# Whole-block transposes of the attention weights inside a matmul half, in a fused attention and recurrent block

## The chip, the cores and the metric

The kernel runs on one core of a Trainium2 chip. The metric is the device time of one execution in microseconds. The core has a matrix engine (TensorE: PE for its matmuls, PEld for its weight loads), three engines for elementwise work (VectorE: DVE, ScalarE: ACT, GpSimd: POOL), a queue engine (SP) that mainly issues DMAs, an on-chip memory (SBUF) of 128 partitions, and an accumulation memory (PSUM) of eight banks. TensorE writes to PSUM alone; DVE and ACT read it.

## The reference

The input is a residual stream of 2048 positions by 1024 channels, all in float32. One projection of 1024 to 9216 columns gives queries, keys and values of 24 heads, gates, and the input of a recurrence. Branch A is causal attention in three groups of eight heads: each query sees the keys of its own block of 128 and of the block before, with the positions regrouped by residue for dilations 1, 4 and 16.

```python
s = jnp.einsum('brnqhd,brnkhd->brnhqk', qb, kw) * (Dh ** -0.5)
s = jnp.where(valid[None, None, :, None], s, NEG_INF)
m = jnp.max(s, axis=-1, keepdims=True)
p = jnp.exp(s - m)
l = jnp.sum(p, axis=-1, keepdims=True)
o = jnp.einsum('brnhqk,brnkhd->brnqhd', p, vw)
...
wts = jax.nn.softmax(jnp.stack(lses, axis=0), axis=0)
attn = jnp.sum(wts[..., None] * jnp.stack(outs, axis=0), axis=0)
...
y_a = attn @ w_attn_proj[l]
...
y_b = (h * jax.nn.silu(g_lru)) @ w_lru_proj[l]
merged = gates[:, :, 0] * y_a + gates[:, :, 1] * y_b
out = merged @ w_out[l] + b_out[l]
x = layer_norm(DEEPNORM_ALPHA * x + out, ln_gain[l], ln_bias[l])
```

Branch B is a convolution, a gated linear recurrence over the positions, and a projection, y_b.

## The kernel before, in words

The kernel has three stages: the input projection with everything that is elementwise behind it; a loop of 49 steps ("groups") with the attention, into which the y_b projection is woven; and the rest of y_b, y_a, the output projection and the normalisation. The change lies in the middle loop alone.

The attention has 12 units (a pair of heads of one dilation), each with 16 query blocks. A block m has, for each of its two heads, a score tile of 128 queries by 256 keys; where a block has no block before it only 128 keys are used. All blocks but the first of dilation 1, and all but the first four of dilation 4, have 256; those of dilation 16 have 128. The prediction calls a group whose blocks have 256 a full group and one with 128 a half group. A group G takes four blocks, 4G to 4G+3, as two pairs, j = 2G and 2G+1. Its steps:

- `scores(j)` (matmul at L975): queries times keys for two blocks and both heads. The two heads lie on the lower and upper 64 partitions, so each matmul has 64 rows. The result goes to two banks of PSUM, tags s0 and s1, two buffers of each.
- `weigh(m)`: for each head a DVE instruction (L987) adds the mask, negates, and takes the extreme, and an ACT instruction (L989) makes the exponential and its sum. The weights p lie in an SBUF tile with eight places.
- `turn_p(j)` (L1003): TensorE transposes p, since the sums need the keys on the partitions. Each 128x128 block is turned in two halves of 64 queries; the halves go to two banks of PSUM, tags t0 and t1, one buffer of each. `copy_p(j, e)` takes a bank to SBUF: t0 on ACT (L1016), t1 on DVE (L1018), or on ACT in groups with spreads for the second pair.
- `values(js)` (L1035): the sums of p times v for two pairs, with 64 columns of the array for each head, into one bank (tag o, one buffer); DVE copies it to the unit's output (L1051).
- `yb_part(n, hf, i)` (L1205): three of the 12 matmuls, 128 by 128 by 512, of one half of the y_b projection's tile n; from group 4 on there is a half in each group but two (the groups after tiles 7 and 15).
- `spread(hp, c, g, tag)` (L1129): a matmul that spreads the shares of the three dilations over the partitions, whose result DVE multiplies into the outputs (o<-o,w). There are 36 in the loop, up to two in a group, in the banks t1 and t0.
- `turn_ml(u)` (L1056): in every fourth group, a transpose of a unit's extremes and sums (128 by 128, bank o), copied by ACT.

Each engine runs its instructions in the order in which the program issues them; semaphores hold an instruction until its inputs are there and its output's buffer has been read. So the order of the calls in the loop is the order on every engine. In a group of before it is: turn of pair 2G-2 (weighed in the group before), scores of 2G, two weighings, scores of 2G+1, turn of 2G-1, two weighings, the sums of pairs 2G-3 and 2G-2, then the y_b half with the spreads inside it.

The transposes of v in the first stage (L366) are whole 128x128 blocks, four to a bank, between the 128x512 matmuls of the projection (L633).

Of the kernel before, what the change touches and what calls it, by code (L numbers as in the profile page):

```python
# [8 lines left out]
F32 = mybir.dt.float32  # L9
F32R = mybir.dt.float32r  # L10
AF = mybir.ActivationFunctionType
# [4 lines left out]
P = 128  # L16
# [15 lines left out]
def hybrid_block_kernel(ctx: ExitStack, tc: tile.TileContext, a: dict, out: bass.AP):  # L32
# [27 lines left out]
    ident = cst.tile([P, P], F32, name="ident")  # L60
# [39 lines left out]
    cur = {}  # L100
# [14 lines left out]
    def run(queue):  # L115
        due = [x for x in queue if x[0] <= now["n"]]
        queue[:] = [x for x in queue if x[0] > now["n"]]
        for _, fn in due:
            fn()
# [806 lines left out]
    def gt(name):  # L926
        return rc_p.tile([P, CH], F32, tag="gt", name=name, bufs=3)
# [50 lines left out]
    def weigh(m):  # L978
        u, n = divmod(m, 16)
        bank, lo = st.pop(("s", m))  # L980
        if n == 0:
            ML[u] = at_p.tile([P, P], F32, tag="ml", name=f"ml{u}", bufs=2)
            pool.memset(ML[u][:, 64:P], 0.0)
        p = PT[:, m % 8]
        for h in range(2):
            mm, ll = (ML[u][:, 32 * k + 16 * h + n:32 * k + 16 * h + n + 1] for k in range(2))
            dve.tensor_tensor_reduce(out=p[:, h, lo:256], in0=bank[h][:, m % 2, lo:256], in1=mask[:, lo:256],  # L987
                                     scale=1.0, scalar=3e38, op0=ALU.add, op1=ALU.min, accum_out=mm)
            act.activation(p[:, h, lo:256], p[:, h, lo:256], AF.Exp, scale=-1.0, bias=mm, accum_out=ll)  # L989
        st["p", m] = (p, lo)  # L990

    def turn_p(j, tag="t"):

        pt = [aps.tile([P, 2, 4, 64], F32, tag=f"{tag}{e}", name=f"pt{e}{j}", bufs=1 if tag == "t" else 2) for e in range(2)]
        ptb = at_p.tile([P, 2, 4, P], F32, tag="pt", name=f"ptb{j}", bufs=3)
        los = []
        for b in range(2):
            p, lo = st.pop(("p", 2 * j + b))
            los.append(lo)
            for h in range(2):  # L1000
                for x in range(lo // P, 2):
                    for e, hs in enumerate((lo_, up_)):
                        pe.transpose(pt[e][:, b, 2 * h + x, :], p[hs, h, x * P:(x + 1) * P], ident[hs, hs])  # L1003
        st["t", j] = (ptb, pt, los)

    def copy_p(j, e):
        ptb, pt, los = st["t", j]
        on_act = e == 0 or (j % 2 and (j + 1) // 2 in spreads)
        whole = los[0] == los[1]
        for b in (slice(0, 2),) if whole else (slice(0, 1), slice(1, 2)):  # L1010
            lo = los[b.start]
            dst, src = ptb[:, b, :, 64 * e:64 * e + 64], pt[e][:, b]
            if lo:
                dst, src = (t.rearrange("p b (h x) f -> p b h x f", x=2)[:, :, :, 1, :] for t in (dst, src))
            if on_act:
                act.activation(dst, src, AF.Copy)  # L1016
            else:
                dve.tensor_copy(dst, src)  # L1018

    def values(js, tag="o"):  # L1020
        o = aps.tile([P, 4, P], F32, tag=tag, name=f"o{js[0]}", bufs=2 if tag == "s0" else 1)
        out = []
        for i, j in enumerate(js):
            u, n0 = divmod(2 * j, 16)
            g, _ = unit(u)
            V = AT_X["v"][:, u % 2]
            ptb, _, los = st.pop(("t", j))
            for b in range(2):
                n = n0 + b
                pv = prev(g, n)  # L1030
                lo = los[b]
                for x in range(lo // P, 2):
                    kb = n if x else pv
                    for h, hs in enumerate((lo_, up_)):
                        pe.matmul(o[hs, 2 * i + b, :], V[:, kb, 64 * h:64 * h + 64], ptb[:, b, 2 * h + x, :],  # L1035
                                  start=(x == lo // P), stop=(x == 1))
            if out and out[-1][0] == u and g != 1:
                out[-1][3] += 2
            else:
                out.append([u, n0, 2 * i, 2])  # L1040
        for u, n0, i, m in out:
            g, _ = unit(u)
            dst = o_tile(u)
            if g == 0:
                dst = dst.rearrange("p (n j) -> p n j", j=P)[:, n0:n0 + m]
            elif g == 1:
                c, r = divmod(n0, 4)
                dst = dst[:, c * CH:(c + 1) * CH].rearrange("p (j r) -> p r j", r=4)[:, r:r + m]
            else:
                dst = dst.rearrange("p (j r) -> p r j", r=16)[:, n0:n0 + m]  # L1050
            dve.tensor_copy(dst, o[:, i:i + m])  # L1051
# [72 lines left out]
    def spread(hp, c, g, tag):  # L1124

        cs = slice(c * CH, (c + 1) * CH)
        os = [o_tile(3 * hp + UG[x])[:, cs] for x in range(3)]
        w = cur["ps"].tile([P, CH], F32, tag=tag, name=f"w{hp}{c}{g}", bufs=cur["wb"])
        pe.matmul(w, sel[:, c // 2, g], WH[c % 2], start=True, stop=True)  # L1129
        tt(dve, os[g], os[g], w, ALU.mult)  # L1130
        if g == 0:
            st["ga", hp, c] = rc(f"ga{hp}{c}")
            sp.dma_start(st["ga", hp, c], ga_scr[hp * P:(hp + 1) * P, cs])
            return

        def join():
            tt(pool, os[0], os[0], os[g], ALU.add)
            if g == 1:
                tt(pool, os[0], os[0], st.pop(("ga", hp, c)), ALU.mult)
                if hp == 3 and c == CO[0]:  # L1140
                    later(1, lambda: split(AT[c][:, 3, 0], AT[c][:, 3, 1], os[0]))
                else:
                    pool.dma_start(at_scr[hp * P:(hp + 1) * P, cs], os[0])

        later(1, join)
# [47 lines left out]
    def yb_part(n, hf, i):  # L1193
        c, f = divmod(n, 8)
        if hf == 0 and i == 0:
            YB["t"] = cur["ps"].tile([P, CH], F32, tag="y", name=f"yb{c}{f}", bufs=cur["yb"])
        w = WL[:, n % 2]
        ks = range(4 * hf, 4 * hf + 4)
        if f == 0 or hf:
            order = [(k, a, b) for k in ks for a, b in ((0, 0), (0, 1), (1, 0))]  # L1200
        else:
            order = [(k, 0, b) for k in ks for b in range(2)] + [(k, 1, 0) for k in ks]
        for m in range(3 * i, 3 * i + 3):
            k, a, b = order[m]
            pe.matmul(YB["t"], w[:, a, k], hx(8 * c + k)[:, b], start=(hf == 0 and m == 0), stop=(hf == 1 and m == 11))  # L1205
# [38 lines left out]
            sp.dma_start(ME[c][:, f], yb_scr[f * P:(f + 1) * P, cs])  # L1244
        YG[i] = ga

    cur.update(wb=1, yb=1, ga=lambda i: gt(f"gA{i}"))
    GY = 4
    halves = list(range(64))
    NG = 48  # L1250
# [56 lines left out]
            spreads.setdefault(e + 7 + (i + (hp < 2)) // 2, []).append((hp, c, g))  # L1307

    rests = set()
    for G in range(NG + 1):  # L1310
        run(late)
        if G < NG:
            if G:
                turn_p(2 * G - 2)
                copy_p(2 * G - 2, 0)
                copy_p(2 * G - 2, 1)
            scores(2 * G)
            weigh(4 * G)
            weigh(4 * G + 1)
            scores(2 * G + 1)  # L1320
            if G:
                turn_p(2 * G - 1)
                copy_p(2 * G - 1, 0)
                copy_p(2 * G - 1, 1)
            weigh(4 * G + 2)
            weigh(4 * G + 3)
            if G:
                values([j for j in (2 * G - 3, 2 * G - 2) if j >= 0])
        else:
            turn_p(2 * G - 2)  # L1330
            copy_p(2 * G - 2, 0)
            copy_p(2 * G - 2, 1)
            turn_p(2 * G - 1, "s")
            copy_p(2 * G - 1, 0)
            copy_p(2 * G - 1, 1)
            values([2 * G - 3, 2 * G - 2])
            values([2 * G - 1], "s0")
        for fn in todo.pop(G, ()):
            fn()
        y = G >= GY and G not in rests and (G < NG or len(halves) % 2)  # L1340
        if y:
            n, hf = divmod(halves[0], 2)
            yb_part(n, hf, 0)
            yb_part(n, hf, 1)
        two = spreads.pop(G, [])
        if len(two) == 2:
            spread(*two[0], "t1")
        if y:
            yb_part(n, hf, 2)
        if two:  # L1350
            spread(*two[-1], "t0")
        if y:
            yb_part(n, hf, 3)
            if hf:
                yb_done(n)
        if G % 4 == 0 and G:
            turn_ml(G // 4 - 1)
        if y:
            yb_care(halves.pop(0))
            if hf and n in (7, 15):  # L1360
                rests.add(G + 1)
        now["n"] += 1
    assert not todo and not spreads, (todo, spreads)
    now["n"] += 1
    run(late)
# [269 lines left out]
```

## Time and profile before

| | |
|---|---|
| median of 3 runs | 2123.78 us (2121.55 to 2124.33) |
| the profiled execution's own time | 2123.79 us |
| its span | 2122.0 us |
| TensorE matmul rows busy | 2099.0 us, 11637 instructions |
| DVE, ACT, POOL busy | 1660.3, 1216.8 and 764.2 us |
| the loop: first scores to the last ml transpose | 1452.6 to 1785.2 us |
| transposes of p in the loop | 1200 rows |

All rows come from one profiled execution. In the lists by line, a row names line, engine, operation, tiles (out<-in), the array rows by columns and the moving operand, and then the count, busy time, mean length of one and the idle time before it. In the order of time a row is start, length, engine, line and so on, with instructions of one kind that follow each other put together. A matmul's length is its latency; several are in flight at a time, so what matmuls cost is read from the starts. A scores or sums matmul has two rows in the trace, a transpose one.

### The profile page before, as it was taken

What the parts mean: (1) busy time and instruction counts of PE and PEld (TensorE: products, weight loads), DVE (VectorE), ACT (ScalarE), POOL (GpSimd) and SP (SyncE); (2) the same over time, 40 slices, a digit from 0 to 9 for tenths busy, and PEclk for the clock granted to TensorE, in tenths of its full rate; (3) what the DMA queues carried; (4) which work ended last, traced back from release to release, by engine and by line L of the source; (5) the groups of instructions that cost most, each with busy time, mean ns of one, the idle gap of its engine ahead of it and who ended that gap; (6) DMA issues with size and microseconds to landing.
All of it is one profiled execution on the core that took longest, in us unless ns stands there. A gap on an engine that the chain in (4) does not pass through costs nothing. (4 is left out here: it accounts for less than half of the span.)

```text
span 2122.0 us, 34703 instructions
## 1 busy us (share of the span) xinstructions
PE 2099.0 (99%) x11637; PEld 1721.6 (81%) x11637; DVE 1660.3 (78%) x2938; ACT 1216.8 (57%) x2502; POOL 764.2 (36%) x692
## 2 busy tenths in 40 slices
PE   9999999999999999999999999999999999999998
PEld 7888888888888888888888888887878788788886
DVE  8787987988989767787677878775777777787667
ACT  6456456467457556677677777676666675321100
POOL 1554654654744301120110111113557678522120
PEclk9999999999999999999999999999999999999999
DMA  7876976976876966676666676769889886774431
GB/s 228 256 222 187 272 225 206 265 224 210 264 230 216 301 189 182 190 206 179 194 199 183 189 229 184 214 194 273 204 214 237 226 229 187 236 240 153 155 99 70
DMA packets 277505, 443.49 MB, mean 209 GB/s; under 512 B 64352, under 2 KB 116608, under 8 KB 274256
## 3 DMA queue, kind: packets, MB, share of 16 engines
q1 hardware_dynamic: 260688, 408.84, 62.8%
q0 software_dynamic: 11744, 23.54, 6.1%
q10 hardware_dynamic: 4896, 8.92, 1.1%
q8 instruction: 92, 1.51, 0.3%
q14 instruction: 85, 0.70, 0.1%
HBM read 290.00 MB, written 151.19 MB: 208 GB/s over the span
## 5 line engine op out<-in xcount | busy, mean ns | idle before, releaser
L633 PE MATMUL q<-xT,hS 128*128 128x512 f32 x1632 | 504.7, 390 | 0.0
L633 PE MATMUL q<-xT,l 128*128 128x512 f32 x1088 | 423.5, 389 | 0.0
L633 PE MATMUL q<-xB,hA 128*128 128x512 f32 x1344 | 417.2, 392 | 0.0
L633 PE MATMUL q<-xB,l 128*128 128x512 f32 x944 | 367.7, 389 | 0.0
L633 PEld LDWEIGHTS q<-xT,hS 128*128 128x128 f32 x1632 | 304.8, 188 | 64.4 <-issue 1.8
L633 PEld LDWEIGHTS q<-xB,hA 128*128 128x128 f32 x1344 | 250.3, 188 | 56.5 <-issue 5.5
L633 PEld LDWEIGHTS q<-xT,l 128*128 128x128 f32 x1088 | 204.3, 188 | 42.5
L236 POOL TENSOR_TENSOR sw<-sw,sin 128x512 f32<-128x512 f32 x96 | 156.1, 1632 | 167.7 <-ACT sw L325 74.0
L633 PEld LDWEIGHTS q<-xB,l 128*128 128x128 f32 x944 | 177.2, 188 | 37.0
L989 ACT ACTIVATE pt<-pt,ml 128x256 f32<-128x256 f32 (+1 forms) x384 | 172.2, 452 | 25.4 <-DVE ml L987 25.4
L236 POOL TENSOR_TENSOR y<-y,h 128x512 f32<-128x512 f32 x28 | 39.1, 1398 | 384.0 <-DVE h L535 368.0
L633 PE MATMUL q<-xB,hS 128*128 128x512 f32 x544 | 168.7, 391 | 1.1 <-DVE v L236 1.1
L633 PE MATMUL q<-xT,hA 128*128 128x512 f32 x544 | 167.9, 390 | 0.0
L280 ACT ACTIVATE hA<-wA 128x512 fp32r<-128x512 f32 x220 | 138.6, 635 | 29.2 <-DVE l L236 11.6
L1205 PE MATMUL yb<-hx,wl 128*128 128x512 f32 x576 | 149.5, 400 | 1.0 <-POOL hx L1181 0.8
L280 ACT ACTIVATE hS<-S 128x512 fp32r<-128x512 f32 x170 | 108.4, 638 | 66.0 <-DVE S L236 47.0
L236 POOL TENSOR_TENSOR l<-wA,hA 128x512 fp32r<-128x512 f32 x68 | 110.1, 1618 | 86.4 <-ACT hA L280 52.5
L1205 PEld LDWEIGHTS yb<-hx,wl 128*128 128x128 f32 x576 | 104.5, 188 | 29.9 <-issue 5.8
L987 DVE CUSTOM_DVE_ANT_0 pt<-s,mask 128x256 f32<-128x256 f32 (+1 forms) x384 | 115.6, 361 | 5.1 <-PE s L975 2.9
L633 PEld LDWEIGHTS q<-xT,hA 128*128 128x128 f32 x544 | 101.8, 188 | 21.7 <-issue 0.4
L633 PEld LDWEIGHTS q<-xB,hS 128*128 128x128 f32 x544 | 101.2, 188 | 22.4 <-issue 1.9
L324 ACT ACTIVATE sw<-y 64x512 f32<-64x512 f32 x96 | 60.6, 631 | 80.6 <-DVE y L577 78.7
(209 smaller groups left out, 4332.1 us busy)
## 6 DMA issues: line engine op xcount, KB each, us to landing
wA<-in_w_in_dram SPq DMA_DIRECT2D x220, 256.0 KB
wl_scr<-l SPq DMA_DIRECT2D x102, 512.0 KB
l<-wl_scr SPq DMA_DIRECT2D x102, 512.0 KB
wS<-in_w_in_dram SPq DMA_DIRECT2D x102, 256.0 KB
wS<-in_w_in_dram POOLq DMA_DIRECT2D x68, 256.0 KB, 6.8
wlr<-in_w_f_dram SPq DMA_DIRECT2D x64, 256.0 KB
mg_scr<-y SPq DMA_DIRECT2D x59, 256.0 KB
v_scr<-vs SPq DMA_DIRECT2D x48, 260.0 KB
```

The lines of the kernel that those rows point to most:

```text
L236: eng.tensor_tensor(out=out, in0=in0, in1=in1, op=op)
L280: act.activation(heads(h), heads(r, False), AF.Copy)
L324: act.activation(flat(sw)[lo_], flat(rw)[up_], AF.Copy, scale=scale)
L633: pe.matmul(bank, w[:, ks], x[:, kk, xx], start=(first and i == 0), stop=(last and i == 11))
L987: dve.tensor_tensor_reduce(out=p[:, h, lo:256], in0=bank[h][:, m % 2, lo:256], in1=mask[:, lo:256], scale=1.0, scalar=3e38, op0=ALU.add, o ...
L989: act.activation(p[:, h, lo:256], p[:, h, lo:256], AF.Exp, scale=-1.0, bias=mm, accum_out=ll)
L1205: pe.matmul(YB["t"], w[:, a, k], hx(8 * c + k)[:, b], start=(hf == 0 and m == 0), stop=(hf == 1 and m == 11))
```

## The change

The diff, without lines that only moved with their block:

```diff
     def turn_p(j, tag="t"):
-        pt = [aps.tile([P, 2, 4, 64], F32, tag=f"{tag}{e}", name=f"pt{e}{j}", bufs=1 if tag == "t" else 2) for e in range(2)]
+        pt = [aps.tile([P, 4, P], F32, tag=f"{tag}{b}", name=f"pt{b}{j}", bufs=1 if tag == "t" else 2) for b in range(2)]
...
                 for x in range(lo // P, 2):
-                    for e, hs in enumerate((lo_, up_)):
-                        pe.transpose(pt[e][:, b, 2 * h + x, :], p[hs, h, x * P:(x + 1) * P], ident[hs, hs])
+                    pe.transpose(pt[b][:, 2 * h + x, :], p[:, h, x * P:(x + 1) * P], ident)
...
-    cur.update(wb=1, yb=1, ga=lambda i: gt(f"gA{i}"))
+    cur.update(wb=2, yb=1, ga=lambda i: gt(f"gA{i}"))
...
+    def turn(j, tag="t"):
+        turn_p(j, tag)
+        copy_p(j, 0)
+        copy_p(j, 1)
...
         if G < NG:
-            if G:
-                turn_p(2 * G - 2)
-                copy_p(2 * G - 2, 0)
-                copy_p(2 * G - 2, 1)
             scores(2 * G)
             weigh(4 * G)
             weigh(4 * G + 1)
             scores(2 * G + 1)
-            if G:
-                turn_p(2 * G - 1)
-                copy_p(2 * G - 1, 0)
-                copy_p(2 * G - 1, 1)
             weigh(4 * G + 2)
-            weigh(4 * G + 3)
-            if G:
-                values([j for j in (2 * G - 3, 2 * G - 2) if j >= 0])
...
+        if G > 1:
+            values([2 * G - 4, 2 * G - 3])
         for fn in todo.pop(G, ()):
             fn()
         if y:
             yb_part(n, hf, 0)
+        if len(two) == 2:
+            spread(*two[0], "s0")
+        if y:
             yb_part(n, hf, 1)
-        if len(two) == 2:
-            spread(*two[0], "t1")
+        if G:
+            turn(2 * G - 2)
+        if G < NG:
+            weigh(4 * G + 3)
         if y:
             yb_part(n, hf, 2)
         if two:
-            spread(*two[-1], "t0")
+            spread(*two[-1], "s1")
         if y:
             yb_part(n, hf, 3)
...
         if G % 4 == 0 and G:
             turn_ml(G // 4 - 1)
+        if G:
+            turn(2 * G - 1, "t" if G < NG else "s")
...
+    values([2 * G - 2, 2 * G - 1])
```

Each 128x128 block of p is turned by one instruction, and the two banks hold the two query blocks of a pair instead of the two halves of the queries. `copy_p` copies a whole bank, so its size and its engines stay. The first turn of a group stands between the second and third part of the y_b half, the second behind the half. The sums take the pairs turned in the group before and follow the scores. The spreads take buffers of the scores' tags s0 and s1, and the fourth weighing of a group stands behind the first turn's copies. Nothing is computed differently, and no DMA is added or taken away.

How that moves the instructions, on TensorE in a full group with a y_b half. Before (o are the sums, yb the half, mlt the turn of ml, pt a turn's banks, s the scores); the pt rows go on alternately up to 16:

```order
L1035 MATMUL o_15174<-ptb_15040,V 64x128 x8
L1035 MATMUL o_15174<-ptb_15104,V 64x128 x8
L1205 MATMUL yb_15195<-hx_13951,wl 128x512 x12
L1056 MATMUL mlt_15208<-ident,ml_14681 128x128
L1003 MATMUL pt_15221<-ident,pt 128x64
L1003 MATMUL pt_15222<-ident,pt 128x64
```

The same place in the change, up to the next scores:

```order
L1031 MATMUL o_14797<-ptb_14743,V 64x128 x4
L1031 MATMUL o_14797<-ptb_14763,V 64x128 x4
L1201 MATMUL yb_14814<-hx_13951,wl 128x512 x6
L1002 MATMUL pt_14821<-ident,pt 128x128 x4
L1002 MATMUL pt_14822<-ident,pt 128x128 x4
L1201 MATMUL yb_14814<-hx_13951,wl 128x512 x6
L1002 MATMUL pt_14844<-ident,pt 128x128 x4
L1002 MATMUL pt_14845<-ident,pt 128x128 x4
L975 MATMUL s_14865<-qk_13830 128x256
```

The turn stands inside the y_b half, eight instructions in two banks, and a second one behind the half; the scores follow it directly.

On DVE, from the third weighing of such a group in the change to the first of the next (L987 are a weighing's two instructions for one head, L1047 copies the sums, L1014 copies a turn's bank):

```order
L987 ISA pt,ml_14573<-s_14788,mask 128x256
L987 ISA ml_14573 128x1
L1047 COPY o_13947<-o_14797 128x2x128 x2
L1014 COPY ptb_14823<-pt_14822 128x512
L987 ISA pt,ml_14573<-s_14787,mask 128x256
L987 ISA ml_14573 128x1
L987 ISA pt,ml_14573<-s_14788,mask 128x256
L987 ISA ml_14573 128x1
L1014 COPY ptb_14846<-pt_14845 128x512
L987 ISA pt,ml_14573<-s_14865,mask 128x256
```

Before, all four weighings of a group stood ahead of the copy of its sums, and no copy of a turn stood between the third and the fourth:

```order
L1018 COPY ptb_15489<-pt_15488 128x8x64
L987 ISA pt,ml_15129<-s_15481,mask 128x256
L987 ISA ml_15129 128x1
L987 ISA pt,ml_15129<-s_15482,mask 128x256
L987 ISA ml_15129 128x1
L987 ISA pt,ml_15129<-s_15481,mask 128x256
L987 ISA ml_15129 128x1
L987 ISA pt,ml_15129<-s_15482,mask 128x256
L987 ISA ml_15129 128x1
L1051 COPY o_13946<-o_15516 128x512
```

The copy of a turn now waits for TensorE between the third and the fourth weighing, and the fourth weighing is queued behind it.

More of the change, by code (lines that the diff above doesn't have):

```diff
@@ L1001, in turn_p, with copy_p @@
                 for x in range(lo // P, 2):
-                    for e, hs in enumerate((lo_, up_)):
-                        pe.transpose(pt[e][:, b, 2 * h + x, :], p[hs, h, x * P:(x + 1) * P], ident[hs, hs])
+                    pe.transpose(pt[b][:, 2 * h + x, :], p[:, h, x * P:(x + 1) * P], ident)
         st["t", j] = (ptb, pt, los)
-    def copy_p(j, e):
+    def copy_p(j, b):
         ptb, pt, los = st["t", j]
[L1008 to L1018, printed above, removed]
+        on_act = b == 0 or (j % 2 and (j + 1) // 2 in spreads)
+        dst, src = ptb[:, b], pt[b]
+        if los[b]:
+            dst, src = (t.rearrange("p (h x) f -> p h x f", x=2)[:, :, 1, :] for t in (dst, src))
+        if on_act:
+            act.activation(dst, src, AF.Copy)
+        else:
+            dve.tensor_copy(dst, src)
     def values(js, tag="o"):
@@ L1309, in hybrid_block_kernel @@
     rests = set()
+    def turn(j, tag="t"):
+        turn_p(j, tag)
+        copy_p(j, 0)
+        copy_p(j, 1)
     for G in range(NG + 1):
         run(late)
+        y = G >= GY and G not in rests and (G < NG or len(halves) % 2)
+        if y:
+            n, hf = divmod(halves[0], 2)
+        two = spreads.get(G, [])
         if G < NG:
-            if G:
-                turn_p(2 * G - 2)
-                copy_p(2 * G - 2, 0)
-                copy_p(2 * G - 2, 1)
             scores(2 * G)
@@ L1320, in hybrid_block_kernel @@
             scores(2 * G + 1)
-            if G:
-                turn_p(2 * G - 1)
-                copy_p(2 * G - 1, 0)
-                copy_p(2 * G - 1, 1)
             weigh(4 * G + 2)
-            weigh(4 * G + 3)
-            if G:
-                values([j for j in (2 * G - 3, 2 * G - 2) if j >= 0])
[L1329 to L1337, printed above, removed]
+        if G > 1:
+            values([2 * G - 4, 2 * G - 3])
         for fn in todo.pop(G, ()):
             fn()
-        y = G >= GY and G not in rests and (G < NG or len(halves) % 2)
         if y:
-            n, hf = divmod(halves[0], 2)
             yb_part(n, hf, 0)
+        if len(two) == 2:
+            spread(*two[0], "s0")
+        if y:
             yb_part(n, hf, 1)
-        two = spreads.pop(G, [])
-        if len(two) == 2:
-            spread(*two[0], "t1")
+        if G:
+            turn(2 * G - 2)
+        if G < NG:
+            weigh(4 * G + 3)
         if y:
@@ L1357, in hybrid_block_kernel @@
             turn_ml(G // 4 - 1)
+        if G:
+            turn(2 * G - 1, "t" if G < NG else "s")
+        spreads.pop(G, None)
         if y:
```

## The prediction

> **What bounds the kernel now.** I read the page first, then the busy time by stretch for the stage with the attention, then the order of time on TensorE for single groups of its loop, then who TensorE waited for.
>
> ```profile
> span 2122.0 us, 34703 instructions
> PE 2099.0 (99%) x11637; PEld 1721.6 (81%) x11637; DVE 1660.3 (78%) x2938; ACT 1216.8 (57%) x2502; POOL 764.2 (36%) x692
> ...
> core 0: us, PE busy (x) PEld busy (x) DVE busy (x) ACT busy (x) POOL busy (x), PEclk, DMA share, GB/s
> 1452.60:1475.60 23.00, 20.69 (x313) 17.16 (x312) 20.28 (x93) 22.14 (x86) 9.55 (x12) 1.00 1.06 313
> 1475.60:1580.40 104.80, 103.73 (x1151) 84.83 (x1151) 69.88 (x305) 69.19 (x283) 53.79 (x82) 1.00 0.83 203
> 1580.40:1785.20 204.80, 199.51 (x2266) 164.21 (x2263) 151.04 (x588) 139.55 (x536) 150.88 (x177) 1.00 0.84 221
> ```
>
> TensorE is busy for 99% of the span, at a granted clock of 1.00. The loop that the change rewrites runs from 1452.6 to 1785.2 us. In the first stretch (groups 0 to 3, no y_b half yet) ACT is as full as TensorE, 22.14 of 23.00. After that ACT and DVE are busy for two thirds to three quarters, and TensorE for all of it but 1.07 and 5.29 us. Its idle time in the whole loop is 2.31 + 1.07 + 5.29 = 8.7 us: that is nearly all that a better order of waits can win. A busy matmul row says little about speed, so the work itself I price by starts. One group with full blocks, on TensorE, from the order of time (start, length, then line and tiles):
>
> ```profile
> 1539.81 0.71 PE L1003 MATMUL pt<-ident,pt 64*128 64x64 f32 x16
> 1540.36 1.95 PE L975 MATMUL s<-qk 64*128 64x256 f32 x16
> 1542.14 0.66 PE L1003 MATMUL pt<-ident,pt 64*128 64x64 f32 x16
> 1542.73 1.97 PE L1035 MATMUL o<-ptb,V 128*64 128x128 f32 x32
> 1544.63 3.03 PE L1205 MATMUL yb<-hx,wl 128*128 128x512 f32 x12
> 1547.59 0.71 PE L1003 MATMUL pt<-ident,pt 64*128 64x64 f32 x16
> ```
>
> From start to start: turn 0.55, scores 1.78, turn 0.59, sums 1.90, y_b half 2.96; the group takes 7.78 us and no row waits. So what a transpose costs TensorE goes straight into the time.
>
> **The turns themselves.** A turn of full blocks is 16 transposes of 64 rows (8 blocks in two halves) before, 8 of 128 rows after. The halves of a block use different rows of the array and go in pairs: 16 of them in 0.55 us, with a change of array shape at the start, so about 0.065 a block. The trace of before has the new form elsewhere, four at a time, in the transposes of v between full-array matmuls, which is just where the change puts them:
>
> ```profile
> 1106.55 0.39 PE L633 MATMUL q<-xT,l 128*128 128x512 f32 x1
> 1106.77 0.62 PE L633 MATMUL q<-xT,hS 128*128 128x512 f32 x2
> 1107.23 0.39 PE L633 MATMUL q<-xT,l 128*128 128x512 f32 x1
> 1107.46 0.60 PE L366 MATMUL vtp<-ident,y 128*128 128x128 f32 x4
> 1107.81 0.71 PE L633 MATMUL q<-xT,hS 128*128 128x512 f32 x2
> 1108.36 0.40 PE L633 MATMUL q<-xT,l 128*128 128x512 f32 x1
> ```
>
> Three 512-wide matmuls without transposes take 1107.23 - 1106.55 = 0.68, or 0.227 each. From 1107.46 to 1108.36 there are 0.90 us for four transposes and two such matmuls, so the transposes take 0.90 - 0.45 = 0.45: 0.11 us each. A whole block therefore costs 0.11 where its two halves cost 0.065. Half the instructions, but each occupies the array alone. Bounds for the unseen operation (p in place of y): from below the pair's 0.065, from above the single transpose of ml further down, 0.20 with its change of shape. Form, type, size and neighbours are those of the v transposes, so I take 0.11.
>
> The page "TensorEngine Tiling (Array Packing)" of the Trainium skill, section Theoretical Speedup, gives up to 2x for two tiles of 64 rows. By that rule alone the new turn takes twice the old one; the rows above make it 1.7 times, so trace and rule point the same way, against the change.
>
> Full group: 16 blocks x 0.11 = 1.76 for 0.55 + 0.59 = 1.14: **+0.62**. A half group (one key block per query block):
>
> ```profile
> 1659.68 1.11 PE L975 MATMUL s<-qk 64*128 64x128 f32 x16
> 1660.63 0.41 PE L1003 MATMUL pt<-ident,pt 64*128 64x64 f32 x8
> 1660.96 1.09 PE L1035 MATMUL o<-ptb,V 128*64 128x128 f32 x16
> ...
> 1666.66 0.47 PE L1003 MATMUL pt<-ident,pt 64*128 64x64 f32 x8
> 1666.96 1.11 PE L975 MATMUL s<-qk 64*128 64x128 f32 x16
> ```
>
> Its turns take 0.33 + 0.30 = 0.63 and become 8 x 0.11 = 0.88: **+0.25**.
>
> **The changes of array shape.** Row names show three shapes: 64*128 (scores, old turns), 128*64 (sums), 128*128 (y_b, spreads, ml, new turns). What a change costs, from a group whose y_b half is followed by another 128*128 operation:
>
> ```profile
> 1529.33 3.02 PE L1205 MATMUL yb<-hx,wl 128*128 128x512 f32 x12
> 1532.19 0.27 PE L1056 MATMUL mlt<-ident,ml 128*128 128x128 f32 x1
> 1532.39 0.59 PE L1003 MATMUL pt<-ident,pt 64*128 64x64 f32 x12
> ```
>
> The same 12 matmuls take 2.86 here and 2.96 ahead of a turn, so leaving the shape costs about 0.10. Before, a group changes three times: y_b to turn, turn to sums, sums to y_b. After, again three times: scores to sums, sums to y_b, last turn to scores. Putting scores and sums side by side saves none. The old y_b to turn goes (-0.10), the old turn to sums was inside the 0.59; new are scores to sums and turn to scores (+0.09 each, as 0.59 against 0.50), and the scores' first weight load, which a turn of the same shape had covered (+0.05). Net **+0.13** a group.
>
> "TensorEngine Tiling (Array Packing)", section Key Properties, says that a change of tiling mode drains TensorE. The trace agrees at 0.10 a time; by this rule the change would gain only if it made fewer changes.
>
> How many groups:
>
> ```profile
> L1003 PE MATMUL pt<-ident,pt 64*128 64x64 f32 x1200 | 56.4, 227 | 5.6 <-DVE o L236 2.0 <-ACT ptb L1016 1.8 <-ACT pt L989 0.4
> L975 PE MATMUL s<-qk 64*128 64x256 f32 x432 | 52.7, 382 | 0.0
> L975 PE MATMUL s<-qk 64*128 64x128 f32 x336 | 24.0, 280 | 0.0
> ```
>
> At 16 rows a group, 432 are 27 full groups and 336 are 21 half ones. TensorE's work grows by 27 x 0.75 + 21 x 0.37 = 20.3 + 7.8 = **28 us**.
>
> **What waiting goes and comes.** Who TensorE waited for in the loop (total, times, longest):
>
> ```profile
> PE pt L1003 <- DVE o L236: 2.0, 2, 1.0
> PE pt L1003 <- ACT ptb L1016: 1.8, 3, 0.9
> PE w L1129 <- DMA wh<-w_scr: 1.1, 1, 1.1
> PE w L1129 <- ACT ptb L1016: 0.9, 1, 0.9
> PE yb L1205 <- POOL hx L1181: 0.8, 1, 0.8
> ```
>
> The two DVE rows and the 0.9 come from spreads in the turns' banks; with the spreads in the scores' banks they go, save that in the two groups without y_b the second turn must wait for the copies of the first. A spread group also hides a short one:
>
> ```profile
> 1607.13 0.84 PE L1205 MATMUL yb<-hx,wl 128*128 128x512 f32 x3
> ...
> 1608.04 0.84 PE L1205 MATMUL yb<-hx,wl 128*128 128x512 f32 x3
> 1608.98 0.28 PE L1003 MATMUL pt<-ident,pt 64*128 64x64 f32 x2
> ```
>
> Three y_b matmuls followed by the turn take 0.94 here, against 0.68 + 0.10: 0.16, in some 13 groups, 2.1 us, gone after. The spread's place in the scores' ring costs nothing: the bank it takes was read by the group's first two weighings, and the next scores take the bank of the last weighing, due well before. The hx wait goes (y_b starts later), the wh one perhaps halves. Together about -6.
>
> New waits: the copy of a turn on ACT and DVE now stands behind six of the group's eight exponentials and weighings, and the fourth weighing behind that copy. Their pace:
>
> ```profile
> 1540.65 0.69 DVE L1018 COPY ptb<-pt 128x512 f32<-128x512 f32 x1
> 1541.48 0.42 DVE L987 CUSTOM_DVE_ANT_0 pt<-s,mask 128x256 f32<-128x256 f32 x1
> 1541.83 0.08 DVE L987 DVE_READ_ACCUMULATOR2_ANT ml<- 128x1 f32 x1
> ...
> 1543.93 0.57 ACT L1016 ACTIVATE ptb<-pt 128x512 f32<-128x512 f32 x1
> 1544.41 0.50 ACT L989 ACTIVATE pt<-pt,ml 128x256 f32<-128x256 f32 x1
> ...
> 1544.90 0.50 ACT L989 ACTIVATE pt<-pt,ml 128x256 f32<-128x256 f32 x1
> ```
>
> In a full group of 8.5 us, six exponentials at 0.49 from about 1.2 end at 4.1; the first turn ends at 6.2 (1.9 + 1.9 + half of y_b 1.4 + 0.9 and edges). ACT is waiting by then; its copy ends at 6.9, and the second turn, which needs the banks, starts at 7.5. DVE weighs the fourth block by 7.6; the next scores need that bank at 9.6. The sums need ACT's second copy at 1.9 of the next group and have it at 0.7. So nothing in the steady state: 0.6 us and more of cover each. Groups 0 to 3 lack the y_b half that gives the cover. In group 1, by the same paces, the first turn ends at about 5.4 us from the loop's start; ACT has done group 0's exponentials at 5.2, six more at 8.1 and the copy at 8.6, and the second turn needs that copy's bank: TensorE stands for 3 us, then a little in groups 2 and 3. I count 5.6 us of waiting before the first y_b, against 3.5 or so (2.31 idle, the rest under modelled ends): +2. The last sums wait alone for the last copy: +1. The two groups without y_b: +1. Net of all waits **-2**; bounds -11 (all 8.7 idle us and the 2.1 go, nothing comes) and +10 (0.2 us in each group).
>
> Sum against the execution's own time: span 2122.0 + 28 - 2 = 2148; the execution took 2123.79, 1.8 more than its span, and the median is 2123.78: **2150**. All TensorE work behind the loop moves back with it.
>
> **Rivals.** (a) The copies end last: if DVE or ACT is 0.6 to 1 us later than I walk it, each full group waits for the copy ahead of its sums or second turn. At 0.4 us in 27 groups: 2150 + 11 = 2161. For it: four queued steps in a row, and the first stretch shows how full ACT is without y_b. Against: ACT 66% and DVE 67 to 74% busy afterwards, and groups get longer. (b) Not slower: if a block's load of weights hid behind its neighbour, as a y_b matmul's does, the whole block would cost 0.065. Then a full group gains 0.1 and loses 0.13, and the waits decide: 2114 to 2124, say 2120. It decides from 0.11 - 26/600 = 0.067 us a block. Against: the 0.11 of the v transposes, in the same surroundings. (c) The order costs the clock: a stand of 3 us in group 1 could lower the granted clock, 1.00 in every stretch so far with stands of at most 1.1 us; some 4 us of work at half rate is +4: 2154. "TensorE: Matmul & The Clock Gate" of the Trainium skill, Part 1, has the clock fall to half after an idle window of about 3.4 us; no run here shows such a stand in the loop.
>
> **Numbers.** Forecast 0.76 (2150, own range 2140 to 2159), (a) 0.12, (b) 0.06, (c) 0.06. A measurement tells 0.2%, about 4 us, from no change. Slower 0.94, same 0.03 and faster 0.03 (the two halves of b). Range 2139 to 2162.
>
> **What would show it.** Right: rows of 8 whole transposes with 0.11 from start to start, a full group of about 8.5 us on TensorE, no idle time ahead of turns in spread groups, the first y_b near 1478. Wrong: whole blocks at 0.065 (b), or sums waiting for copies in group after group (a), or a granted clock under 1.00 near 1460 (c).

## The result and the profile after

| | before | the change |
|---|---|---|
| median | 2123.59 us (2121.55 to 2124.33, 4 runs) | 2148.41 us (2146.78 to 2148.73, 4 runs) |
| the profiled execution, its span | 2123.79, 2122.0 us | 2148.36, 2146.6 us |

The ratio is 1.0116, with a 95% interval of 1.01 to 1.0132: the change costs 24.8 us. The forecast was 2150, with a range of 2139 to 2162.

The page of the change, and the busy time by stretch for the three stretches that answer to those of before (groups 0 to 3, then the two parts of the rest of the loop; the columns are those of the prediction's first lines):

```profile
span 2146.6 us, 33530 instructions
PE 2127.4 (99%) x11037; PEld 1747.3 (81%) x11037; DVE 1655.5 (77%) x2926; ACT 1223.3 (57%) x2498; POOL 764.3 (36%) x692
...
1452.60:1479.50 26.90, 23.02 (x220) 18.50 (x219) 18.45 (x85) 21.15 (x80) 14.11 (x17) 0.94 1.05 305
1479.50:1592.00 112.50, 112.26 (x987) 92.99 (x986) 71.89 (x305) 71.17 (x281) 49.45 (x77) 1.00 0.73 182
1592.00:1812.10 220.10, 218.66 (x1919) 180.18 (x1917) 150.80 (x585) 145.59 (x543) 153.35 (x179) 1.00 0.81 209
```

TensorE runs 600 rows fewer and is busy longer. From group 4 on it now stands for only 0.24 and 1.44 us, against 1.07 and 5.29 before; the first stretch stands for 3.88 us against 2.31, and at a mean clock of 0.94. So the waits got better almost everywhere, and the time went up all the same. One full group without spreads, TensorE in order of time (start, length, line and tiles):

```profile
1523.61 2.00 PE L975 MATMUL s<-qk 64*128 64x256 f32 x16
1525.54 1.97 PE L1031 MATMUL o<-ptb,V 128*64 128x128 f32 x32
1527.44 1.66 PE L1201 MATMUL yb<-hx,wl 128*128 128x512 f32 x6
1528.93 1.04 PE L1002 MATMUL pt<-ident,pt 128*128 128x128 f32 x8
1529.72 1.63 PE L1201 MATMUL yb<-hx,wl 128*128 128x512 f32 x6
1531.20 1.03 PE L1002 MATMUL pt<-ident,pt 128*128 128x128 f32 x8
1532.16 0.38 PE L975 MATMUL s<-qk 64*128 64x128 f32 x2
```

From start to start: scores 1.93, sums 1.90, y_b 1.49, turn 0.79, y_b 1.48, turn 0.96 with the change of array shape to the next scores; 8.55 in all, against 7.78 before. The two turns take 1.75 us where the pairs of 64-row halves took 1.14. A half group:

```profile
1497.11 1.16 PE L975 MATMUL s<-qk 64*128 64x128 f32 x16
...
1500.72 0.60 PE L1002 MATMUL pt<-ident,pt 128*128 128x128 f32 x4
1501.07 1.62 PE L1201 MATMUL yb<-hx,wl 128*128 128x512 f32 x6
1502.54 0.60 PE L1002 MATMUL pt<-ident,pt 128*128 128x128 f32 x4
1503.06 1.16 PE L975 MATMUL s<-qk 64*128 64x128 f32 x16
```

It takes 5.95 us from scores to scores, its neighbours 5.95 to 5.98 without a turn of ml, against 5.58 before; I count 5.96. Over 27 full and 21 half groups that is 27 x 0.77 + 21 x 0.38 = 28.8 us of added TensorE work.

The start of the loop in the change, on TensorE, with the idle time and its releaser in brackets:

```profile
1457.29 0.87 PE L1002 MATMUL pt<-ident,pt 128*128 128x128 f32 x6
1461.19 1.70 PE L1002 MATMUL pt<-ident,pt 128*128 128x128 f32 x8 [3.02 <-ACT ptb L1012]
1462.82 3.02 PE L975 MATMUL s<-qk 64*128 64x256 f32 x16
...
1479.46 1.66 PE L1201 MATMUL yb<-hx,wl 128*128 128x512 f32 x6
```

The second turn of group 1 stands for 3.02 us behind ACT's copy. Then 8 transposes take 1.63 us from start to start instead of 0.79, and the 16 rows of scores after them, 3.02 long in the list, have 2.00 in the full group above: about half speed. The granted clock, by stretches of 1 us, says so too:

```profile
1461.00:1462.00 1.00, 0.81 (x5) 0.81 (x6) 0.00 (x0) 1.00 (x5) 0.00 (x0) 0.76 1.03 301
1462.00:1463.00 1.00, 1.00 (x7) 0.67 (x7) 0.08 (x1) 0.67 (x3) 0.00 (x0) 0.50 0.99 260
1463.00:1464.00 1.00, 1.00 (x6) 0.83 (x8) 0.61 (x1) 0.00 (x0) 0.00 (x0) 0.50 1.05 348
1464.00:1465.00 1.00, 1.00 (x8) 0.83 (x6) 0.00 (x0) 0.00 (x0) 0.00 (x0) 0.53 1.04 369
```

From 1465 on it is 1.00 again. The clock lacks 0.24 + 0.50 + 0.50 + 0.47 = 1.71 us of full speed, which is 3.4 us at half. Who TensorE waited for in the loop of the change (total, times, longest), the whole list:

```profile
PE pt L1002 <- ACT ptb L1012: 5.1, 8, 3.0
PE w L1125 <- DMA wh<-w_scr: 0.4, 1, 0.4
```

From group 4 on, five of the eight waits for ACT's copies are left, 1.2 us. Two of them, 0.24 and 0.19 us, are in the two groups without y_b. The other three, 0.24, 0.29 and 0.28, are in full groups without spreads, which take 8.99 to 9.04 us instead of 8.55. There ACT stands for POOL ahead of the copy, in a step that makes the shares of the three dilations (L1098), as this row sums up (total, times, longest):

```profile
ACT mt L1098 <- POOL mt L236: 6.8, 3, 2.3
```

Last, what stands behind the loop: the first y_b matmul there and the first of y_a, before and then in the change, and the weight loads of the spreads in between.

```profile
1785.26 0.48 PE L1205 MATMUL yb<-hx,wl 128*128 128x512 f32 x1
1851.27 0.39 PE L1477 MATMUL ya<-at,wa 128*128 128x512 f32 x1
...
PEld w L1129 <- DVE o L236: 3.6, 7, 1.0
```

```profile
1812.11 0.50 PE L1201 MATMUL yb<-hx,wl 128*128 128x512 f32 x1
1875.49 0.39 PE L1470 MATMUL ya<-at,wa 128*128 128x512 f32 x1
...
PEld w L1125 <- DVE o L236: 0.8, 2, 0.4
```

The piece shrinks from 66.0 to 63.4 us. The loop itself, from the first scores (1452.62 and 1452.64) to these rows, grows from 332.6 to 359.5. So the span's +24.6 is +26.8 in the loop and -2.6 behind it, and the rest comes at the end. Below, pieces of the loop are always taken from the first scores on: in the profiled executions of this study these start between 1450.1 and 1453.3 us, though what stands ahead of the loop is not edited in any kernel.

### The profile page after: what moved, and what is told of

The parts are those of the page before. It is cut to its first block, busy times and chain, and to the rows that moved or that the text cites. A ratio compares the mean times of both kernels' runs of the same rounds, so it can differ in the third digit from the quotient of the medians.

```text
span 2146.6 us, 33530 instructions
## 1 busy us (share of the span) xinstructions
PE 2127.4 (99%) x11037; PEld 1747.3 (81%) x11037; DVE 1655.5 (77%) x2926; ACT 1223.3 (57%) x2498; POOL 764.3 (36%) x692
## 3 DMA queue, kind: packets, MB, share of 16 engines
q1 hardware_dynamic: 260688, 408.84, 62.5%
q8 instruction: 88, 1.44, 0.3%
## 4 chain that ended last, share of the span: by engine, by line
PE 59%; issue 2%; POOL 2%; DMA 2%; ACT 1%; DVE 1%; SPq 0%; POOLq 0%; DVEq 0%; ACTq 0%
PE q L633 33%; PE yb L1201 6%; PE z L1505 3%; PE z L1503 3%; PE z L1504 3%; PE s L975 2%; PE o L1031 2%; PE pt L1002 2%; PE ya L1471 1%; PE ya L1472 1%; PE ya L1470 1%; PE g L494 1%; ACT pt L989 1%; DMA wor<-in_w_out_dram 1%; DMA atr<-at_scr 1%
## 5 line engine op out<-in xcount | busy, mean ns | idle before, releaser
L1201 PE MATMUL yb<-hx,wl 128*128 128x512 f32 x576 | 159.6, 407 | 0.0
L987 DVE CUSTOM_DVE_ANT_0 pt<-s,mask 128x256 f32<-128x256 f32 (+1 forms) x384 | 116.9, 361 | 26.5 <-PE s L975 24.6
```

## The experiments

The theory is the prediction's: the change pays with the price of a whole block, 0.11 us against 0.065, on TensorE, which has no idle time to hide it, and the new order is nearly even. The rivals: that the order (its waits, its changes of shape) is what costs, that whole blocks are not dearer, and that the clock is.

**One half of the change at a time.** First the new order with the old turns:

```diff
-        pt = [aps.tile([P, 4, P], F32, tag=f"{tag}{b}", ...) for b in range(2)]
+        pt = [aps.tile([P, 2, 4, 64], F32, tag=f"{tag}{e}", ...) for e in range(2)]
...
-                    pe.transpose(pt[b][:, 2 * h + x, :], p[:, h, x * P:(x + 1) * P], ident)
+                    for e, hs in enumerate((lo_, up_)):
+                        pe.transpose(pt[e][:, b, 2 * h + x, :], p[hs, h, x * P:(x + 1) * P], ident[hs, hs])
```

(`copy_p` is that of before as well.)

> The new order (turns inside and behind the y_b half, sums one group on, spreads in the scores' banks), but each 128x128 block of p turned in two 64-row halves as before. Theory (the form of the transposes makes the loss): 8 pairs take 0.50 us instead of 0.88. The first turn now leaves and re-enters the full array shape inside the half (about 0.33 us of edges with the weight loads), the second saves the edge ahead of the scores. Full group about 0.43 us shorter than in the change, half group 0.05: 27 x 0.43 + 21 x 0.05 = 12.7, so about 2136 us. Rival (the order makes the loss): 2148 or more.

Measured: 2136.11 us (2134.22 to 2136.95, 4 runs), ratio to before 1.0059 (1.0046 to 1.0073). TensorE in order of time:

```profile
1550.93 0.71 PE L1003 MATMUL pt<-ident,pt 64*128 64x64 f32 x16
1551.48 1.95 PE L975 MATMUL s<-qk 64*128 64x256 f32 x16
1553.36 1.97 PE L1035 MATMUL o<-ptb,V 128*64 128x128 f32 x32
1555.26 1.66 PE L1205 MATMUL yb<-hx,wl 128*128 128x512 f32 x6
1556.85 0.71 PE L1003 MATMUL pt<-ident,pt 64*128 64x64 f32 x16
```

With 64-row turns inside and behind the y_b half, a group changes the array's shape five times instead of three. By these starts it takes 1.88 + 1.90 + 1.59 + 0.64 + 1.59 + 0.55 = 8.15 us (the 0.55 from the two rows ahead), 0.37 more than before, so about 0.18 for each of the two more changes. The new order suits the old turns badly: +12.5 us of the 24.8 without a single whole block.

Then the old order with whole blocks (the reverse of the edit above, in the kernel before):

> The order of before with whole-block transposes, the only part of the change that is left. Theory: the transposes cost 27 x 0.76 + 21 x 0.38 = 28 us more, and since the turns next to the scores now have another shape, a group makes four changes of shape instead of three, 0.14 us with the weight loads, 48 x 0.14 = 7: about 2159 us, slower than the change itself. Rival (the order makes the loss): about 2124 us. Rival (the form alone, changes of shape are free): about 2150 us.

Measured: 2153.26 us (2152.96 to 2155.55, 4 runs), ratio 1.0144 (1.013 to 1.0158).

```profile
1553.90 2.00 PE L975 MATMUL s<-qk 64*128 64x256 f32 x16
1555.83 1.10 PE L1002 MATMUL pt<-ident,pt 128*128 128x128 f32 x8
1556.85 1.97 PE L1031 MATMUL o<-ptb,V 128*64 128x128 f32 x32
1558.75 3.02 PE L1201 MATMUL yb<-hx,wl 128*128 128x512 f32 x12
1561.61 1.03 PE L1002 MATMUL pt<-ident,pt 128*128 128x128 f32 x8
1562.57 0.60 PE L975 MATMUL s<-qk 64*128 64x128 f32 x6
```

A full group takes 1562.57 - 1553.90 = 8.67 us, 0.89 more than before: 0.62 of it the prediction's price of 16 blocks. The remaining 0.27 goes with a fourth change of shape (scores to turn, turn to sums, sums to y_b, turn to scores); what else is in it was not taken apart. The expectation was 6 us too high. The trace places that: the loop grew from 332.6 to 364.9 us, 32.2 where I had 35.2, since TensorE's listed waits fell from 7.0 to 3.3 us; dearer transposes fill time in which it would wait, for ACT's copies (2.7 to 1.0 us) and for hx and wh (1.9 us to nothing). A further 1.3 are missing behind the loop, and this execution entered the loop 1.7 us earlier than that of before.

The two runs together settle what the change is made of. Whole blocks cost 2148.41 - 2136.11 = 12.3 us in the new order and 2153.26 - 2123.59 = 29.7 in the old one; the new order costs 12.5 with halves and -4.9 with whole blocks. That the parts do not add up goes with the changes of shape: halves have three a group in the old order and five in the new, whole blocks four and three. The starts of a full group leave 8.15 + 8.67 - 7.78 - 8.55 = 0.49 us for these three changes, 0.16 each, and half groups (5.95 and about 6.10 in these two runs) about as much. The medians leave 12.5 + 29.7 - 24.8 = 17.4 us, or 0.36 for each of 48 groups. That is less than 0.49, and the four kernels differ in their waits and in groups 0 to 3 as well; that part was not taken apart. The new order also holds the moved spreads, which are worth some 4 us by themselves, as a run below shows. So the rival that whole blocks are not dearer is out, and "the order costs" is true of halves alone.

**The disputed price by itself.** In the change, each whole transpose is issued twice into the same place; in the kernel before, each pair of halves:

```diff
-                    pe.transpose(pt[b][:, 2 * h + x, :], p[:, h, x * P:(x + 1) * P], ident)
+                    for _ in range(2):
+                        pe.transpose(pt[b][:, 2 * h + x, :], p[:, h, x * P:(x + 1) * P], ident)
...
-                    for e, hs in enumerate((lo_, up_)):
+                    for e, hs in 2 * tuple(enumerate((lo_, up_))):
```

> The change, with each whole-block transpose of p made twice in a row into the same place (the output is the same): 600 more of them, nothing else. Theory (0.11 us each, alone on the array): about 66 us more than the change, less some 4 us in groups 0 to 3 where ACT is late anyway: about 2211 us. Rival (a whole block is as cheap as its pair of halves, 0.0625, and the loss has another cause): about 2184 us.

> Before, with each pair of half-block transposes made twice in a row into the same place (the output is the same): 1200 more rows in 600 pairs. Theory (0.0625 us a pair): about 37 us more than before, less some 2 to 3 us in groups 0 to 3: about 2158 us. Rival (a pair takes as long as a whole block, 0.11): about 2186 us.

Measured, one execution each: 2208.8 us with the whole blocks twice, 60.4 over the change's own profiled run, which was taken at another time, and 2152.42 with the pairs twice, 31.1 over the kernel before taken beside it (2121.29). In both, 600 blocks more. TensorE with whole blocks twice, and then with pairs twice:

```profile
1589.68 1.91 PE L1003 MATMUL pt<-ident,pt 128*128 128x128 f32 x16
1591.34 1.63 PE L1202 MATMUL yb<-hx,wl 128*128 128x512 f32 x6
```

```profile
1553.33 1.21 PE L1003 MATMUL pt<-ident,pt 64*128 64x64 f32 x32
1554.38 1.95 PE L975 MATMUL s<-qk 64*128 64x256 f32 x16
```

Sixteen whole transposes take 1.66 us where eight take 0.79: 0.87 for eight more, **0.109 us a block**. Sixteen pairs take 1.05 where eight take 0.55: 0.50 for eight more, **0.0625 us a block**. Those prices hold the whole change: 600 x (0.109 - 0.0625) = 28 us. By them alone the two runs would have risen by 65 and 37.5 us; they rose by 60.4 and 31.1, 5 and 6 less. Part of that is the start of the loop: up to the first y_b, 46 whole blocks more added 3.2 us (5.0 by the price) and 62 pairs more 2.0 us (3.9), the rest filling waits for ACT. Later waits are filled too: the list of what TensorE waited for in the loop falls from 5.5 to 2.4 us with whole blocks twice, and from 7.0 to 3.4 with pairs twice, and the three full groups of 9 us in the change take no longer than their neighbours once the blocks come twice (10.3 us all). As each price comes from one execution, the two distances of starts, which repeat from group to group, are what it rests on.

The page "TensorEngine Tiling (Array Packing)" of the Trainium skill, section Theoretical Speedup, gives up to 2x for two 64-row tiles side by side; these runs show 0.109 / 0.0625 = 1.74. That gain the change gives away.

**The spreads alone.** The kernel before, with only the place of the spreads changed (and the second buffer for wh that the change also has):

```diff
-    cur.update(wb=1, yb=1, ga=lambda i: gt(f"gA{i}"))
+    cur.update(wb=2, yb=1, ga=lambda i: gt(f"gA{i}"))
...
-            spread(*two[0], "t1")
+            spread(*two[0], "s0")
...
-            spread(*two[-1], "t0")
+            spread(*two[-1], "s1")
```

> Before, with one part of the change alone: the spreads take buffers of the scores' tags, so that the next turn does not wait for DVE to have read them. Theory: the 0.16 us in some 13 groups and the longer waits in the two groups without a y_b half go: 2 to 4.5 us less, about 2120 us. Rival (the copies or the exponentials end just as late): 2123 to 2124 us.

Measured: 2119.01 us (2116.41 to 2123.71, 11 runs) against 2123.3 (2120.98 to 2125.97, 15 runs), ratio 0.9981 (0.9972 to 0.999). A turn in a spread group, and the longest row of TensorE's waits in the loop:

```profile
1607.65 0.84 PE L1205 MATMUL yb<-hx,wl 128*128 128x512 f32 x3
1608.43 0.71 PE L1003 MATMUL pt<-ident,pt 64*128 64x64 f32 x16
...
PE pt L1003 <- ACT ptb L1016: 2.8, 4, 0.9
```

The turn starts 0.78 us after its three y_b matmuls instead of 0.94, and no turn waits for DVE's product any more (2.0 us before). This part of the change is the good one: it beats both kernels by itself. Some of its gain may be the second buffer for wh, whose wait fell from 1.1 to 0.6 us; the two were not taken apart.

**The start of the loop.** The change, with the old order where groups have no y_b half (GY is 4): the two turns ahead of and behind the scores, and the fourth weighing straight behind the third.

```diff
         if G < NG:
+            if G and G < GY:
+                turn(2 * G - 2)
             scores(2 * G)
...
             scores(2 * G + 1)
+            if G and G < GY:
+                turn(2 * G - 1)
             weigh(4 * G + 2)
+            if G < GY:
+                weigh(4 * G + 3)
...
-        if G:
+        if G >= GY:
             turn(2 * G - 2)
-        if G < NG:
+        if GY <= G < NG:
             weigh(4 * G + 3)
...
-        if G:
+        if G >= GY:
             turn(2 * G - 1, "t" if G < NG else "s")
```

> The change, but groups 0 to 3 (no y_b half yet) turn p where before did, ahead of and behind the scores, so that the copies on ACT stand behind four exponentials instead of six. Theory (the stand of 3 us in group 1 and the clock that fell after it are part of the loss): first y_b matmul about 3.7 us earlier than in the change and the granted clock 1.00 throughout, about 2144.5 us. Rival (ACT's exponentials bound the start in any order): 2148 us.

Measured: 2142.81 us (2141.78 to 2143.8, 4 runs), ratio to before 1.0092 (1.0078 to 1.0106), 5.6 us less than the change. Order of time on TensorE, and the granted clock by stretch:

```profile
1459.97 1.09 PE L1002 MATMUL pt<-ident,pt 128*128 128x128 f32 x8 [1.29 <-ACT ptb L1012]
1475.48 1.66 PE L1201 MATMUL yb<-hx,wl 128*128 128x512 f32 x6
...
1456.00:1460.00 4.00, 2.71 (x25) 2.03 (x21) 3.21 (x13) 4.00 (x17) 0.00 (x0) 1.00 0.98 286
1460.00:1464.00 4.00, 4.00 (x34) 3.20 (x34) 2.94 (x15) 3.63 (x14) 0.00 (x0) 1.00 1.02 297
```

The longest stand is 1.29 us and the clock stays at 1.00. The first y_b comes 23.5 us after the first scores (1451.94), against 26.8 in the change and 23.0 before: stand and clock together cost the change 3.3 us there. Of the 4.9 us by which the two spans differ, the remaining 1.6 are 0.7 of an earlier entry into the loop, 0.7 behind the loop, where this kernel's spreads wait for nothing, and 0.2 elsewhere.

## Why the prediction was right, and where it was not

- **The turns.** Right: 0.11 a block was read off the transposes of v, which are another tile in another stage, and the measured prices are 0.109 and 0.0625 (forecast 0.065). The row was a good stand-in for an operation that the loop before did not hold. Rival (b), whole blocks at 0.065, is out.
- **The changes of shape.** Right in count and near in size: three a group before and after, and a full group of 8.55 us against 8.53 from the steps, a half group 5.96 against 5.95. The scores take 1.93 us from start to start where they took 1.78, 0.15 for the +0.09 and +0.05 that the prediction gives them. What changes of shape are worth shows in the run with halves in the new order, where two more cost 0.37 a group.
- **The sum of TensorE work.** 28 us forecast, 28.8 by the same groups in the trace of the change.
- **What waiting goes.** The two DVE rows, the hx row and the short hidden waits went as said; wh went from 1.1 to 0.4. The run with the spreads alone (and the second wh buffer) shows that this is a gain by itself, 4.3 us of the median. In its trace the loop takes 329.9 us against 332.6, and the piece behind it 64.6 against 66.0.
- **What waiting comes.** The 3 us stand in group 1 was forecast and came, 3.02, behind ACT's copy as said. Mis-sized was its price: the first y_b came 3.8 us later than before and not 2, at 1479.46 instead of near 1478, since the clock fell behind the stand. That is rival (c), which I had given as a case of its own and which is part of the outcome: 1.71 us of speed lost, where I had counted +4 for it. Of the waits that I put at the last sums and at the two groups without y_b, +1 each, the last sums wait for nothing, and the two groups for 0.24 and 0.19.
- **Rival (a)**, copies that end last in each group: not in each. Apart from the stand in group 1, TensorE waits for copies seven times for 2.1 us in all, and from group 4 on five times for 1.2. But in the three full groups of 9 us it is what happens: they lose 0.44 to 0.49 us each by the starts, about the 0.4 that the rival names. The walk of ACT's steps in the prediction left out L1098, which stands ahead of the copy there.
- **The end.** The step that failed is "all TensorE work behind the loop moves back with it". It moved back by 26.8 us at its beginning and by 24.2 at y_a, because the spreads behind the loop, which waited 3.6 us for DVE before, wait 0.8 after. In six kernels the piece less that wait is the same within 0.4 us: before 66.0 - 3.6 = 62.4; the change 63.4 - 0.8 = 62.6; spreads alone 64.6 - 2.0 = 62.6; old order at the start 62.7 - 0; halves in the new order 63.2 - 0.4 = 62.8; whole blocks in the old one 64.9 - 2.4 = 62.5. So the waits are where the 2.6 us went; why DVE is there in time in some of these kernels was not tried.

In sum: forecast 28 - 2 = +26 on the span, measured +24.6, as +28.8 of work, -3.1 of idle time in the loop (8.67 to 5.56), -2.1 of short waits hidden under modelled ends, +1.7 of clock, -2.6 behind the loop. That makes 22.7. Of the 1.9 that are missing, 0.6 lie in the three full groups of 9 us, which lose 1.4 by the starts and show 0.8 of it as idle; the rest I cannot put on single rows. That 2150 and 2148.4 lie so close is in part luck: against the forecast there are 0.8 us more of work, 3.2 less of waiting, 1.7 more for the clock, 2.6 less behind the loop and these 1.9, and they nearly cancel.

## What to carry to other kernels

Fewer instructions are not less time on a matrix engine that is already full: price an instruction by the distance of starts in the same surroundings, and here two half-height transposes side by side beat one whole one by 1.74. Count the changes of array shape for each pairing of form and order, since a form can be cheap in one order and dear in another, and take out of a rewrite the part that stands by itself: moving the spreads' banks, with a second buffer for wh, was worth 0.2%, and the rest of the change buried it.

## What the runs showed of the hardware

A stand of 3.02 us on TensorE was enough to halve its granted clock, and so was one of 2.37 us in the run with whole blocks twice; stands of 1.29 us and less left it at 1.00. With whole blocks twice the clock lacks 1.71 us of full speed between 1460 and 1465 us, as much as in the change, and the 16 transposes behind the stand take 3.44 us from start to start instead of 1.66:

```profile
1460.99 3.51 PE L1003 MATMUL pt<-ident,pt 128*128 128x128 f32 x16 [2.37 <-ACT ptb L1013]
1464.43 2.00 PE L975 MATMUL s<-qk 64*128 64x256 f32 x16
```

In the change the fall came only after work had started again, at some 1461.5 us, 3.4 us after the stand's beginning, and lasted 3.4 us; with whole blocks twice it came at 1460.8, 2.2 us after the beginning. With halves in the new order the same stand was 3.6 us long. There the fall came at 1456.8, 1.6 us after the beginning, and the clock was 0.60 and 0.55 in the two stretches of 4 us from 1456 and 1460, that is 4 x 0.40 + 4 x 0.45 = 3.4 us of full speed lacking, twice as much (part of it in the stand itself):

```profile
1456.00:1460.00 4.00, 1.18 (x18) 1.19 (x20) 0.93 (x5) 3.78 (x17) 0.00 (x0) 0.60 1.02 308
1460.00:1464.00 4.00, 4.00 (x24) 3.19 (x25) 2.56 (x12) 2.21 (x8) 0.61 (x1) 0.55 1.03 339
```

"TensorE: Matmul & The Clock Gate" of the Trainium skill, Part 1, has the clock at half after an idle window of about 3.4 us, watched in windows of that length that run freely. The runs agree on half speed and on the length, 3.4 us in the change and about twice that with halves, and a fall 1.6 to 3.4 us after the stand's beginning fits windows that do not start with it. But the stands that brought it on were shorter, down to 2.37 us, so a stand cannot be called safe because it is under 3.4. What lies between 1.29 and 2.37 us no run here shows.

A change of array shape in mid-stream cost about 0.10 us by the starts before, and about 0.18 in the run with two more of them. There the first weights of y_b behind a turn load at 1557.49 us, when their matmul starts; in the kernel before, the weights of the scores behind a turn of the same shape load at 1540.30, 0.06 us ahead of their matmul. How much of the 0.18 this is was not measured.
